# A conformer trunk step on one core: three projection tiles take un-normalised tokens

## The chip, the cores and the metric

The kernel runs on one core of a Trainium2 chip. The metric is device time of one execution in microseconds (us). Engines are named as in the profile: PE multiplies matrices, DVE, ACT and POOL work elementwise, SP issues most of the transfers.

## The reference

The program is one step of a two-layer encoder trunk (D = 1024 channels, 512 prompt tokens and 8 x 16 sample tokens, all in F32). Layer 0 is a conformer convolution module and a SwiGLU feed-forward net, layer 1 is attention and a feed-forward net. Only the start of layer 0 is touched by the change:

```
def rms_norm(x, g):
    return x * rsqrt(mean(x * x, axis=-1) + EPS) * g

def conv_module(h, hist, g, w_pw1, b_pw1, w_dw, b_dw, ln_g, ln_b, w_pw2, b_pw2):
    a, gate = split(rms_norm(h, g) @ w_pw1 + b_pw1, 2)
    glu = a * sigmoid(gate)
    full = concat([hist, glu])
    y = depthwise_conv(full, w_dw) + b_dw          # width 31, causal
    y = silu(layer_norm(y, ln_g, ln_b))
    return h + y @ w_pw2 + b_pw2, full[-30:]
```

The root `rsqrt(...)` is one number per token and the gain `g` one number per channel, so the root may be applied before the product with `w_pw1` or to its result.

## The kernel before

Channels lie on the partitions, tokens on the free axis. The 640 tokens are two groups: group 0 has 256 (the samples and the prompt's first 128), group 1 has 384. Each F32 product is made of three matmuls on halves that are split off (`mm3`, L167-172): high weight by high token (L170), low weight by high token (L171), high weight by low token (L172). Weights come through `wsplit` (L128-156): a transfer on SP into `raw`, the high half `whi` by ACT (L150), the low half `wlo` = raw - whi by DVE and POOL (L154). Each of these tiles has two buffers.

Group 0's normalisation (`rms`, L237-246, by `rstd_bc`, L221-231): eight squares, of which ACT makes four (L179) and DVE four (L182); DVE adds them up (L195); PE sums over the channels (L204, tile `w`, a PSUM tile named w2 in the code); DVE adds EPS (L226, `rst`), POOL takes the root (L230), PE spreads it over the partitions (L216). Then for each of the eight channel blocks DVE makes the normalised `n` (L243), ACT its high half (L159), DVE its low half (L160); both are tiles `x`. POOL does group 1's squares and sums; from there its normalisation is the same.

The order of the work is a list of steps, PLAN: "a0 y a1 a2 a4 x a3 a5 a6 l04 p04 l05 d0213 a7 b0 p05 b1 l07 p07 l06 b2 q00 s0 p06 n0 b3 b4 b5 d145 l13 w0 b7 r0 ...". `a`c is the gated projection `glu` (L369-396) of channel block c for group 0: two output tiles `mm` of 24 matmuls each (L170-172), tanh (L380) and identity (L383) on ACT, the gate product on DVE (L386) into the tile `gs`. `b`c is the same for group 1 (gate product L395 into `gp`). The depthwise convolution is made in three ways. `d` is on DVE, one multiply-add for each of 31 taps (L434, L437), into PSUM (`w`). `q` is on ACT and POOL (L409-417; POOL's add is L417). `l` and `p` are on PE: `l` writes a block of `gs` to DRAM (tile `sc`, L452) and reads it back with four shifts (tile `x4`, in the profile `x<-sc`, L455), beside a table `w4` that POOL makes (L444); `p` is then 64 matmuls (L469). `n0` is group 0's layer norm (`conv_ln`, L474-494): sums for the mean, then squares on ACT (L179), adds on POOL (L195), PE's sum (L204), the root (L226, L230), the spread (L216), and eight multiplies on DVE (L489), SiLU (L491) and split (L159, L160) that give the tokens of `w0`, the second projection `pw2` (its results are added to h at L506). `y` loads group 1's tokens, `x` normalises them, `r0` is the next normalisation of group 0, `f` a part of the feed-forward net.

A scheduler with a cost model makes from this list, the data dependences, the priorities (`tc.high_priority`) and the buffers one fixed order of instructions for each engine. An engine takes its instructions in that order and waits where one isn't ready, so a shift of one step can reorder others far behind it.

Of the kernel before, what the change touches and what calls it, by code (L numbers as in the profile page):

```python
# [71 lines left out]
V_NCONV, V_BPW1, V_BDW, V_LNG, V_LNB, V_BPW2 = 0, 8, 24, 32, 40, 48  # L72
# [5 lines left out]
def tile_trunk(ctx, tc, xT, vecs, hist, w_pw1, w_pw2, w_in0, w_out0, w_in1, w_out1,  # L78
               w_kq, w_v, w_o, rel, kc, vc, y_out, convp_out, convs_out, k_out, v_out):
    nc = tc.nc  # L80

    cst = ctx.enter_context(tc.tile_pool(name="cst", bufs=1))
# [37 lines left out]
    bca = cst.tile([P, NT], F32, name="bca", tag="bca")  # L120
# [4 lines left out]
    def col(base, i):  # L125
        return vec[:, base + i:base + i + 1]
# [94 lines left out]
    def rstd_bc(pieces, n, engs=SQ, cut=CUT, r2=None, eng=nc.gpsimd):  # L221
        st = w2t()
        nt = n // P
        r, v = colmean(st, [lambda s=s, e=e: square(s, n, e) for s, e in zip(pieces, engs)], n,
                       cut, "rst", eng)
        last["rst"] = nc.vector.tensor_scalar(out=r[:, :nt], in0=v, scalar1=EPS, scalar2=None,  # L226
                                              op0=ALU.add)
        if r2 is None:
            r2 = tp.tile([P, 4], F32, tag="rst2", name=nm("rst2"))
        nc.gpsimd.tensor_tensor(out=r2[:, :nt], in0=r[:, :nt], in1=mhalf[:, :nt], op=ALU.pow)  # L230
        return spread(st, r2, n), r2

    def hp(g, k):
        g0, n = GR[g]
        return h[:, k, g0:g0 + n]

    def rms(g, gain, engs=SQ, cut=CUT, eng=nc.gpsimd):  # L237
        n = GR[g][1]
        bc, _ = rstd_bc([hp(g, k) for k in range(KT)], n, engs, cut, None, eng)
        xh, xl = new_xs(g)  # L240
        for k in range(KT):
            t = tp.tile([P, 384], F32, tag="n1", name=nm("n1"), bufs=NB1)
            nc.vector.scalar_tensor_tensor(out=t[:, :n], in0=hp(g, k), scalar=col(gain, k),  # L243
                                           in1=bc, op0=ALU.mult, op1=ALU.mult)
            xsplit(t[:, :n], xh[:, k, :], xl[:, k, :])
        return xh, xl, None, None
# [21 lines left out]
    def xk(x, ks):  # L268
        return [(x[0][:, k, :], x[1][:, k, :]) for k in ks]
# [90 lines left out]
         cp.tile([P, KT, 384], F32, name="y1", tag="y")]  # L360

    w00 = wsplit(w_pw1[0], 16, P, cuts=4, pool=PL1[0][0])
    with tc.high_priority(offset=2 * HP):
        xs = [rms(0, V_NCONV, SSQ, SCUT, nc.vector), None]
    load_hist(0, 2)
    w01 = wsplit(w_pw1[1], 16, P, cuts=C01, pool=PL1[0][1])
    nc.scalar.dma_start(dwv, vecs[:, V_N:])

    def glu(c, g, wh, wl):  # L369
        n = GR[g][1]  # L370
        ps = []
        for ab in range(2):
            pt = mmt()
            mm3(pt[:, :n], [(wh[:, (ab * 8 + k) * P:(ab * 8 + k + 1) * P],
                             wl[:, (ab * 8 + k) * P:(ab * 8 + k + 1) * P]) for k in range(KT)],
                xk(xs[g], range(KT)))
            ps.append(pt[:, :n])
        with tc.high_priority(offset=HP):
            t = tp.tile([P, 384], F32, tag="t1", name=nm("t1"))
            nc.scalar.activation(out=t[:, :n], in_=ps[1], func=AF.Tanh, scale=0.5,  # L380
                                 bias=hb1[:, KT + c:KT + c + 1])
            a = tp.tile([P, 384], F32, tag="t2", name=nm("t2"))
            nc.scalar.activation(out=a[:, :n], in_=ps[0], func=AF.Identity, scale=0.5,  # L383
                                 bias=hb1[:, c:c + 1])
            if g == 0:
                nc.vector.scalar_tensor_tensor(  # L386
                    out=gs[:, c, :, HIST:SEG], in0=t[:, :n].rearrange("p (s w) -> p s w", w=SB),
                    scalar=1.0, in1=a[:, :n].rearrange("p (s w) -> p s w", w=SB),
                    op0=ALU.add, op1=ALU.mult)
                nc.gpsimd.tensor_copy(gs[:, c, 9:16, 14:30], gs[:, c, 8:15, 30:46])  # L390
                nc.gpsimd.tensor_copy(gs[:, c, 10:16, 0:14], gs[:, c, 8:14, 32:46])
                nc.gpsimd.tensor_copy(gp[:, c, 14:30], gs[:, c, 15, 30:46])
                nc.gpsimd.tensor_copy(gp[:, c, 0:14], gs[:, c, 14, 32:46])
            else:
                nc.vector.scalar_tensor_tensor(out=gp[:, c, HIST:HIST + 384], in0=t[:, :n], scalar=1.0,  # L395
                                               in1=a[:, :n], op0=ALU.add, op1=ALU.mult)
# [169 lines left out]
    xs = [rms_late(0, None), rms_late(1, None)]  # L566
# [280 lines left out]
    for p in range(NP):  # L847
# [424 lines left out]
```

## Time and profile before

| | us |
|---|---|
| median of 3 runs | 1551.79 (1549.15 to 1553.39) |
| profiled execution | 1551.3 |
| its span | 1549.5 |
| what lies around the span | 1.8 |
| PE busy in the span | 1471.7 (95%) |
| DVE busy | 1050.1 (68%) |
| ACT busy | 662.4 (43%) |
| POOL busy | 443.8 (29%) |

The granted TensorE clock has a mean of 0.984. A row of the timeline reads: start in the span, us from start to the end of its last instruction, engine (SPq is SP's queue of transfers), line, operation, result <- inputs, shapes, number of instructions in a row; in brackets the engine's idle time ahead of it and what ended that. Buffer numbers are left out of names, so `mm`, `x`, `w`, `raw` are each many tiles. A row of the windows reads: from:to, length, busy time and number of instructions of PE, PEld, DVE, ACT and POOL, granted clock, share of the time that transfers ran, GB/s.

### The profile page before, as it was taken

The page shows a single profiled execution, that of the slowest core. Times are in us where ns is not written, and L with a number is a line of the kernel's source. Part 1 is how long each engine was busy: PE and PEld are TensorE (multiplying, and loading weights), DVE is VectorE, ACT ScalarE, POOL GpSimd, SP SyncE. Part 2 cuts the span into 40 slices and gives each one's busy share as a digit, 9 for nine tenths or more (in the row PEclk, how much of TensorE's full clock was granted, in tenths as well). Part 3 has the DMA queues.
Part 4 walks back from the last instruction along what each step waited for, and adds up shares of the span by engine and source line. Part 5 has one row for each costly group of instructions (what it writes and reads, how often), then busy time and mean ns, then how long its engine had stood idle before and what let it go on. Part 6 is the DMA issues. An engine that isn't in the chain of part 4 may idle for free.

```text
span 1549.5 us, 26569 instructions
## 1 busy us (share of the span) xinstructions
PE 1471.7 (95%) x10770; PEld 1398.9 (90%) x10770; DVE 1050.1 (68%) x1863; ACT 662.4 (43%) x1173; POOL 443.8 (29%) x403
## 2 busy tenths in 40 slices
PE   5888998989999999999999999999989999999997
PEld 5878888989999999999988798886989999999997
DVE  6994999988555455457576767566796476476455
ACT  4544454535423323235454445443554244244244
POOL 6865568877501000001321211110411121121110
PEclk9999999999999999999999999998999999999998
DMA  7784434444421333433655545453103213213211
GB/s 236 234 228 142 137 113 159 148 157 153 147 82 55 129 116 129 135 118 126 202 183 201 174 140 205 133 175 114 55 28 109 82 56 109 82 55 109 82 55 68
DMA packets 59658, 199.95 MB, mean 129 GB/s; under 512 B 10128, under 2 KB 22672, under 8 KB 46736
## 3 DMA queue, kind: packets, MB, share of 16 engines
q1 hardware_dynamic: 59248, 197.96, 39.1%
q8 instruction: 84, 1.38, 0.4%
q10 hardware_dynamic: 288, 0.31, 0.1%
q14 instruction: 38, 0.31, 0.1%
HBM read 187.02 MB, written 11.22 MB: 128 GB/s over the span
## 4 chain that ended last, share of the span: by engine, by line
PE 71%; DVE 16%; ACT 3%; issue 3%; DMA 3%; POOL 2%; SPq 0%; POOLq 0%; DVEq 0%; ACTq 0%
PE mm L170 12%; PE mm L172 12%; PE mm L171 12%; PE pb L968 6%; DVE w L437 5%; DVE wlo L154 4%; PE pc L968 4%; PE pa L968 4%; PE pb L170 1%; PE pb L171 1%; PE pb L172 1%; PE pa L172 1%; PE pa L170 1%; PE pc L170 1%; PE pc L172 1%
## 5 line engine op out<-in xcount | busy, mean ns | idle before, releaser
L171 PE MATMUL mm<-x,wlo 128*128 128x256 f32 (+1 forms) x1344 | 416.8, 312 | 15.4 <-DVE wlo L154 14.9
L170 PE MATMUL mm<-x,whi 128*128 128x256 f32 (+1 forms) x1344 | 413.3, 312 | 6.4 <-ACT x L159 3.7
L172 PE MATMUL mm<-x,whi 128*128 128x256 f32 (+1 forms) x1344 | 412.7, 311 | 0.5
L150 ACT ACTIVATE whi<-raw 128x2048 fp32r<-128x2048 f32 (+2 forms) x117 | 197.7, 1694 | 232.6 <-PE mm L172 138.8
L171 PEld LDWEIGHTS mm<-x,wlo 128*128 128x128 f32 x1344 | 257.1, 192 | 18.7 <-DVE wlo L154 17.5
L170 PEld LDWEIGHTS mm<-x,whi 128*128 128x128 f32 x1344 | 254.5, 191 | 11.2 <-ACT x L159 4.1
L172 PEld LDWEIGHTS mm<-x,whi 128*128 128x128 f32 x1344 | 255.1, 191 | 2.9 <-DVE x L160 1.8
L154 DVE TENSOR_TENSOR wlo<-raw,whi 128x2048 fp32r<-128x2048 f32 (+5 forms) x117 | 214.0, 1832 | 62.2 <-ACT whi L150 61.2
L154 POOL TENSOR_TENSOR wlo<-raw,whi 128x1536 fp32r<-128x1536 f32 (+3 forms) x50 | 145.7, 2918 | 69.0 <-ACT whi L150 69.0
L913 POOL TENSOR_TENSOR raw<-raw 128x512 f32<-128x512 f32 x38 | 50.5, 1330 | 332.3 <-DVE raw L913 257.5
L171 PE MATMUL mm<-hid,wlo 128*128 128x256 f32 (+1 forms) x352 | 107.7, 308 | 6.6 <-DVE wlo L154 6.6
L172 PE MATMUL mm<-hid,whi 128*128 128x256 f32 (+1 forms) x352 | 105.8, 307 | 0.2
L170 PE MATMUL mm<-hid,whi 128*128 128x256 f32 (+1 forms) x352 | 104.6, 307 | 0.1
L437 DVE SCALAR_TENSOR_TENSOR w<-gp,dwv,w 128x384 f32<-128x384 f32 x180 | 103.9, 612 | 0.8
L195 POOL TENSOR_TENSOR acc<-sq,sq 128x384 f32<-128x384 f32 (+1 forms) x8 | 8.1, 1006 | 258.2 <-ACT sq L179 258.1
L171 PEld LDWEIGHTS mm<-hid,wlo 128*128 128x128 f32 x352 | 66.0, 188 | 7.8 <-DVE wlo L154 7.8
L417 POOL TENSOR_TENSOR y<-y,cvt 128x256 f32<-128x256 f32 (+1 forms) x60 | 69.3, 1154 | 6.3 <-ACT cvt L416 4.0
L172 PEld LDWEIGHTS mm<-hid,whi 128*128 128x128 f32 x352 | 65.7, 188 | 0.6 <-DVE hid L160 0.6
L159 ACT ACTIVATE whi<-raw 128x1024 fp32r<-128x1024 f32 x38 | 39.4, 1054 | 61.6 <-PE pc L172 18.1
L170 PEld LDWEIGHTS mm<-hid,whi 128*128 128x128 f32 x352 | 65.2, 188 | 0.4 <-ACT hid L159 0.3
L968 PE MATMUL pa<-x0f,whi 128*128 128x320 f32 x228 | 61.2, 316 | 2.5 <-DVE t L913 2.3
L195 POOL TENSOR_TENSOR acc<-acc,sq 128x384 f32<-128x384 f32 (+1 forms) x48 | 52.7, 1097 | 28.9 <-ACT sq L179 27.5
(317 smaller groups left out, 3391.4 us busy)
## 6 DMA issues: line engine op xcount, KB each, us to landing
raw<-in_w_in SPq DMA_DIRECT2D x62, 1024.0 KB
raw<-in_w_out SPq DMA_DIRECT2D x36, 768.0 KB
raw<-in_w_pw SPq DMA_DIRECT2D x22, 1024.0 KB
cache<-in_ck SPq DMA_DIRECT2D x32, 512.0 KB
cache<-in_cv SPq DMA_DIRECT2D x32, 512.0 KB
raw<-in_w_kq SPq DMA_DIRECT2D x8, 1024.0 KB
x<-sc SPq DMA_DIRECT2D x16, 368.0 KB
raw<-in_w_out SPq DMA_DIRECT2D x4, 1024.0 KB
```

Source lines behind the costliest of these rows:

```text
L150: nc.scalar.activation(out=hi[:, a:b], in_=raw[:, a:b], func=AF.Copy)
L154: eng.tensor_tensor(out=lo[:, a:b], in0=raw[:, a:b], in1=hi[:, a:b].bitcast(F32), op=ALU.subtract)
L159: nc.scalar.activation(out=hi, in_=src, func=AF.Copy)
L170: nc.tensor.matmul(ps, wh, xh, start=(i == 0), stop=False)
L171: nc.tensor.matmul(ps, wl, xh, start=False, stop=False)
L172: nc.tensor.matmul(ps, wh, xl, start=False, stop=(i == last))
L195: last["acc"] = eng.tensor_tensor(out=acc[:, :n], in0=prev, in1=s(), op=ALU.add)
L417: nc.gpsimd.tensor_tensor(out=y[g][:, c, :], in0=y[g][:, c, :], in1=pr[:, :n], op=ALU.add)
L437: nc.vector.scalar_tensor_tensor(out=dst, in0=src, scalar=wj, in1=dst, op0=ALU.mult, op1=ALU.add)
L913: ENG[e].tensor_tensor(out=out, in0=a, in1=b, op=op)
L968: nc.tensor.matmul(ps, a[:, c], b[:, k, :], start=(first and k == 0 and i == 0), stop=(k == 3 and i == 2), skip_group_check=not first)
```

## The change

All eight of group 0's squares are now on ACT. The projection tiles a0, a1 and a2 no longer take `x` but a new tile `xr`: the tokens times the gain, split into halves by eight ACT and eight DVE instructions, without the root. It lies in the buffer that group 1's `x` gets later. ACT copies the spread roots from PSUM into `bca`, and the six results of a0, a1, a2 are multiplied by it on DVE on their way from PSUM to tanh and identity. The normalised `x` of group 0 is still made, for a3 to a7. Lines of the changed kernel are 1 to 18 higher than those of the kernel before: L171 is L170 before, L205 is L204, L217 is L216, L180 is L179, L399 is L380, L401 is L383, L470 and L473 are L452 and L455; new are L242 (copy of the roots), L370 and L372 (split of `xr`), L397 (the multiplies).

```diff
-SSQ = 'avavavav'
+SSQ = 'aaaaaaaa'
+RAW = (0, 1, 2)
...
-    def rms(g, gain, engs=SQ, cut=CUT, eng=nc.gpsimd):
+    def rms(g, gain, engs=SQ, cut=CUT, eng=nc.gpsimd, keep=None):
...
+        if keep is not None:
+            nc.scalar.activation(out=keep, in_=bc, func=AF.Copy)
...
+    xr = cst.tile([P, 2, KT, 384], F32R, tag="x1", name="xr")
+    xr = xr[:, 0, :, 0:256], xr[:, 1, :, 0:256]
+    with tc.high_priority(offset=4 * HP):
+        for k in range(KT):
+            nc.scalar.activation(out=xr[0][:, k, :], in_=hp(0, k), func=AF.Copy,
+                                 scale=col(V_NCONV, k))
+            nc.vector.scalar_tensor_tensor(out=xr[1][:, k, :], in0=hp(0, k),
+                                           scalar=col(V_NCONV, k),
+                                           in1=xr[0][:, k, :].bitcast(F32), op0=ALU.mult,
+                                           op1=ALU.subtract)
     with tc.high_priority(offset=2 * HP):
-        xs = [rms(0, V_NCONV, SSQ, SCUT, nc.vector), None]
+        xs = [rms(0, V_NCONV, SSQ, SCUT, nc.vector, bca[:, 0:256]), None]
...
+        raw = g == 0 and c in RAW
...
-                xk(xs[g], range(KT)))
+                xk(xr if raw else xs[g], range(KT)))
...
+            if raw:
+                for i, o in ((1, t), (0, a)):
+                    nc.vector.tensor_tensor(out=o[:, :n], in0=ps[i], in1=bca[:, 0:n], op=ALU.mult)
+                    ps[i] = o[:, :n]
```

At the program's start PE's order before is the sum and the spread of the roots, then a0 (results `mm_28`, `mm_29`) and a1 (`mm_32`, `mm_33`) in turn, block by block of the normalised `x_16`:

```order
L204 MATMUL w2_4_123<-onec_80,acc_6_126 128x1 x2
L216 MATMUL w2_4_123<-ident_75,rst2_15_152 128x128 x2
L170 MATMUL mm_28_210<-x_16_156,whi_2_109 128x256
L171 MATMUL mm_28_210<-x_16_156,wlo_3_110 128x256
L170 MATMUL mm_29_235<-x_16_156,whi_2_109 128x256
L171 MATMUL mm_29_235<-x_16_156,wlo_3_110 128x256
L170 MATMUL mm_32_271<-x_16_156,whi_26_191 128x256
L171 MATMUL mm_32_271<-x_16_156,wlo_27_192 128x256
L170 MATMUL mm_33_296<-x_16_156,whi_26_191 128x256
L171 MATMUL mm_33_296<-x_16_156,wlo_27_192 128x256
L172 MATMUL mm_28_210<-x_16_156,whi_2_109 128x256
```

In the changed kernel PE starts with a0 on `xr`, and from its 36th row on the order reads (rows in between left out):

```order
L171 MATMUL mm_28_228<-xr_123,whi_2_109 128x256
L172 MATMUL mm_28_228<-xr_123,wlo_3_110 128x256
L173 MATMUL mm_28_228<-xr_123,whi_2_109 128x256
...
L172 MATMUL mm_29_253<-xr_123,wlo_3_110 128x256
L205 MATMUL w2_4_140<-onec_80,acc_6_143 128x1 x2
L173 MATMUL mm_29_253<-xr_123,whi_2_109 128x256
...
L173 MATMUL mm_32_291<-xr_123,whi_26_209 128x256
L217 MATMUL w2_4_140<-ident_75,rst2_15_169 128x128 x2
L171 MATMUL mm_32_291<-xr_123,whi_26_209 128x256
```

The sum of the roots moved behind 35 matmuls and the spread behind 66 of them (and the sum): both stood at the head of the queue. The multiplies of a0 and the normalised tokens, which a4 is the first to take, follow the spread.

On SP the four shifted reads of l04 (`x4`, L455 before) stood behind the transfer of a7's weights and now stand ahead of it.

Further on, on ACT around the second part of n0 (squares `sq_172` to `sq_180`; `t1_211` is the tanh of b5's gate, `whi_223` the high half of weights that come later). Before:

```order
L380 ACTIVATE t1_204_1562<-mm_203_1537,hb1_85 128x384
L150 ACTIVATE whi_218_1703<-raw_217_1702 128x2048
L179 ACTIVATE sq_178_1386<-y0_106 128x256
L179 ACTIVATE sq_179_1389<-y0_106 128x256
L383 ACTIVATE t2_212_1625<-mm_209_1573,hb1_85 128x384
L179 ACTIVATE sq_180_1392<-y0_106 128x256
L380 ACTIVATE t1_211_1623<-mm_210_1598,hb1_85 128x384
L150 ACTIVATE whi_223_1762<-raw_222_1761 128x2048
L491 ACT_TABLE_LOAD
L491 ACTIVATE n1_184_1405<-y0_106,vec_73 128x256
```

In the changed kernel the same place reads:

```order
L401 ACTIVATE t2_212_1648<-mm_209_1597,hb1_85 128x384
L180 ACTIVATE sq_175_1401<-y0_106 128x256
L180 ACTIVATE sq_176_1404<-y0_106 128x256
L180 ACTIVATE sq_177_1407<-y0_106 128x256
L180 ACTIVATE sq_178_1410<-y0_106 128x256
L399 ACTIVATE t1_211_1647<-mm_210_1622,hb1_85 128x384
L151 ACTIVATE whi_223_1786<-raw_222_1785 128x2048
L180 ACTIVATE sq_179_1413<-y0_106 128x256
L180 ACTIVATE sq_180_1416<-y0_106 128x256
L509 ACT_TABLE_LOAD
L509 ACTIVATE n1_184_1429<-y0_106,vec_73 128x256
```

The last two squares, which stood ahead of b5's tanh and of `whi_223`, now stand behind both. POOL's queue has the same change: `wlo_224`, its part of the low half of those weights, stood behind the root of n0 and now stands ahead of its last two adds. Before, and then in the changed kernel:

```order
L154 TENSOR_TENSOR wlo_219_1704<-raw_217_1702,whi_218_1703 128x1024
L195 TENSOR_TENSOR acc_173_1373<-acc_173_1373,sq_178_1386 128x256
L195 TENSOR_TENSOR acc_173_1373<-acc_173_1373,sq_179_1389 128x256
L195 TENSOR_TENSOR acc_173_1373<-acc_173_1373,sq_180_1392 128x256
L230 TENSOR_TENSOR rst2_182_1399<-rst_181_1397,mhalf_82 128x2
L154 TENSOR_TENSOR wlo_224_1763<-raw_222_1761,whi_223_1762 128x1024
```

```order
L196 TENSOR_TENSOR acc_173_1397<-acc_173_1397,sq_177_1407 128x256
L196 TENSOR_TENSOR acc_173_1397<-acc_173_1397,sq_178_1410 128x256
L155 TENSOR_TENSOR wlo_224_1787<-raw_222_1785,whi_223_1786 128x1024
L196 TENSOR_TENSOR acc_173_1397<-acc_173_1397,sq_179_1413 128x256
L196 TENSOR_TENSOR acc_173_1397<-acc_173_1397,sq_180_1416 128x256
L231 TENSOR_TENSOR rst2_182_1423<-rst_181_1421,mhalf_82 128x2
L155 TENSOR_TENSOR wlo_229_1846<-raw_227_1844,whi_228_1845 128x1024
```

The sum (PE), the root (DVE and POOL), the spread (PE) and the eight multiplies on DVE (L489) come behind those adds in both kernels. Of the work that stands ahead of these multiplies on DVE, the changed kernel has in addition three of group 1's convolution steps (L437 before) and one DVE part of `wlo_224`. Between the first `n` of group 1 and a7's gate product DVE has 14 convolution steps of group 0 and 2 other gate products, where it had 18 and 3. From the feed-forward net on, the orders are alike on every engine.

More of the change, by code (lines that the diff above doesn't have):

```diff
@@ L379, in glu @@
             t = tp.tile([P, 384], F32, tag="t1", name=nm("t1"))
+            a = tp.tile([P, 384], F32, tag="t2", name=nm("t2"))
+            if raw:
+                for i, o in ((1, t), (0, a)):
+                    nc.vector.tensor_tensor(out=o[:, :n], in0=ps[i], in1=bca[:, 0:n], op=ALU.mult)
+                    ps[i] = o[:, :n]
             nc.scalar.activation(out=t[:, :n], in_=ps[1], func=AF.Tanh, scale=0.5,
                                  bias=hb1[:, KT + c:KT + c + 1])
-            a = tp.tile([P, 384], F32, tag="t2", name=nm("t2"))
             nc.scalar.activation(out=a[:, :n], in_=ps[0], func=AF.Identity, scale=0.5,
```

## The prediction

> **What bounds the kernel now.** The page's first line is read first. PE is busy for 95% of the span, so what costs time is what makes PE wait; the rest is for the stages to say.
>
> ```profile
> PE 1471.7 (95%) x10770; PEld 1398.9 (90%) x10770; DVE 1050.1 (68%) x1863; ACT 662.4 (43%) x1173; POOL 443.8 (29%) x403
> ```
>
> The windows view then cuts the span where something is handed on: from the first `n` of group 1 to the gate of a7, from p07 to the end of b5, from the multiplies of n0 to 326 us, and from 400 us to the end.
>
> ```profile
> 51.77:81.41 29.64, 24.53 (x223) 21.96 (x222) 29.57 (x42) 17.20 (x30) 24.80 (x29) 0.94 0.92 240
> 103.81:149.10 45.29, 44.56 (x334) 40.19 (x334) 26.04 (x46) 14.19 (x23) 20.57 (x17) 0.96 0.49 136
> 152.00:326.00 174.00, 155.63 (x1226) 147.50 (x1226) 173.22 (x289) 86.58 (x122) 123.81 (x66) 0.96 0.43 140
> 400.00:1549.50 1149.50, 1126.16 (x8054) 1073.53 (x8053) 704.74 (x1325) 465.92 (x883) 162.83 (x192) 0.99 0.34 114
> ```
>
> PE is not the bound everywhere. In the first stage DVE works 29.57 of 29.64 us and PE waits for it; in the second PE works 44.56 of 45.29; in the third DVE 173.22 of 174. From 400 us on PE works 98% of the time in an unchanged order, so I take that part to be handed on as it is, only earlier or later. The change happens in the first 40 us, and what counts is what reaches 400 us through two stages that DVE bounds.
>
> **The start: PE is earlier, the roots are later.** The timeline of the first 45 us:
>
> ```profile
> 9.89 4.58 ACT L150 ACTIVATE whi<-raw 128x512 fp32r<-128x512 f32 x8
> ...
> 11.11 1.28 DVE L154 TENSOR_TENSOR wlo<-raw,whi 128x512 fp32r<-128x512 f32 x2
> ...
> 15.03 1.22 PE L216 MATMUL w<-ident,rst 128*128 128x128 f32 x4 [1.17 <-POOL rst L230]
> ...
> 16.29 0.87 DVE L243 SCALAR_TENSOR_TENSOR n<-h,vec,w 128x256 f32<-128x256 f32 x2 [1.21 <-PE w L216]
> ...
> 17.27 0.58 PE L170 MATMUL mm<-x,whi 128*128 128x256 f32 x1 [1.02 <-ACT x L159]
> 17.65 0.41 PE L171 MATMUL mm<-x,wlo 128*128 128x256 f32 x1
> 17.86 0.41 PE L170 MATMUL mm<-x,whi 128*128 128x256 f32 x1
> ...
> 22.57 0.28 PE L170 MATMUL mm<-x,whi 128*128 128x256 f32 x1
> 22.69 0.28 PE L171 MATMUL mm<-x,wlo 128*128 128x256 f32 x1
> ```
>
> Before, PE starts a0 at 17.27, behind the roots. Un-normalised tokens need only h and the gain: eight ACT and eight DVE instructions. The same forms on `x` give their prices:
>
> ```profile
> 16.80 0.81 ACT L159 ACTIVATE x<-n 128x256 fp32r<-128x256 f32 x2 [2.33 <-DVE n L243]
> ...
> 17.93 2.01 DVE L160 TENSOR_TENSOR x<-n,x 128x256 fp32r<-128x256 f32 x2
> ...
> 23.08 0.82 DVE L160 TENSOR_TENSOR x<-n,x 128x256 fp32r<-128x256 f32 x2
> ```
>
> That is 8 x 0.405 = 3.2 us of ACT and 8 x 0.41 = 3.3 us of DVE, up to 8 x 1.0 = 8.0 where the splits run as slowly as at 17.93. ACT has four more squares ahead of or among the weights as well. The first high half of weights moves from 9.89 to about 11.4 and the first low half, which PE needs at its second matmul, is ready at about 13.1 (11.11 + 0.68 for one of that pair + 1.3 for the `xr` splits ahead of it). So PE starts at 13.1 in place of 17.27: 4.2 us earlier, with bounds of 2 and 5.9 (first high half at 11.4, or the slow splits). For the first 5.3 us matmuls follow each other every 0.21 us (17.65, 17.86), from 22.57 on every 0.12; this slow beginning moves along and costs the same.
>
> What it costs is the root. Its sum now stands behind 35 matmuls and its spread behind 67 rows of PE. So the sum runs at about 20 (13.1, then 25 matmuls in the slow 5.3 us and 10 more at 0.12), and the spread, after 31 more at 0.12, at about 24, not 15.03. The normalised tokens start at 24.1, not 16.29: 7.8 us later.
>
> ```profile
> 36.01 0.38 PE L171 MATMUL mm<-x,wlo 128*128 128x256 f32 x1 [0.42 <-POOL wlo L154]
> ...
> 40.87 1.92 ACT L150 ACTIVATE whi<-raw 128x2048 fp32r<-128x2048 f32 x1 [1.45 <-DMA raw<-in_w_pw]
> ...
> 44.63 0.39 PE L170 MATMUL mm<-x,whi 128*128 128x256 f32 x2
> ...
> 51.77 1.13 DVE L243 SCALAR_TENSOR_TENSOR n<-h,vec,w 128x384 f32<-128x384 f32 x2
> ```
>
> Before, a2's second half waits for a low half at 36.01, ACT waits for the transfer of weights at 40.87, and a3 starts at 44.63. a0 and a1 now end at about 28 (96 matmuls from 13.1: 25 in 5.3 us, 71 at 0.12, and some 1.2 for the sum and the spread). But a2's weights go through ACT, DVE and POOL, and on ACT their high half (1.9) stands behind the first results of a0 and a1, which need the roots in `bca` (one ACT copy out of PSUM, about 0.48 like the tanh at 149.14 below, hidden beside DVE) and the first three multiplies, so it starts after 26. I take 31 to 33 for the low half, and a2 still ends near 36: the start's 4 us are spent there. a4 is the first that needs normalised tokens. From 24.1 DVE has eight `n` (0.435 each), eight low halves (0.41 to 1.0), six multiplies from PSUM (each about an `n`, 0.435: 2.6 us; bounds 0.36, a third of the 1.08 at 151.67 below, and 1.0, as at 17.93) and weight splits; by these durations the last low half is there at 39.4. PE waits in a4's first half until about 39.8, a4 ends at about 44.0 against 44.63, and the first `n` of group 1 comes 0.3 us earlier, at about 51.5. The four DVE squares removed (4 x 0.42) are paid for by six multiplies.
>
> **The first DVE stage: 2.4 us earlier.** The timelines of PE, DVE and SP:
>
> ```profile
> 67.03 5.24 PE L469 MATMUL mm<-x,w 128*32 128x256 f32 x64 [5.11 <-DMA x<-sc]
> ...
> 103.81 5.62 PE L469 MATMUL mm<-x,w 128*32 128x256 f32 x64 [5.43 <-DMA x<-sc]
> ```
>
> ```profile
> 80.16 0.55 DVE L160 TENSOR_TENSOR x<-n,x 128x384 fp32r<-128x384 f32 x1
> ...
> 81.41 0.41 DVE L386 SCALAR_TENSOR_TENSOR gs<-t,t 128x256 f32<-128x256 f32 x1
> ```
>
> ```profile
> 82.87 1.42 SPq L452 DMA_DIRECT2D sc<-gs  x2
> ...
> 91.74 1.74 SPq L455 DMA_DIRECT2D x<-sc  x4
> ```
>
> With the shifted reads of l04 ahead of a7's weights, p04's wait of 5.11 us at 67.03 goes. But b0 then needs group 1's tokens, the last low half of which DVE makes at 80.16, and p07 needs the gate of a7 (DVE, 81.41), the write at 82.87 and the reads at 91.74, which land when p07 starts at 103.81. That chain hangs on DVE. Ahead of a7's gate DVE has four convolution steps and one gate fewer:
>
> ```profile
> L437 DVE SCALAR_TENSOR_TENSOR w<-gs,dwv,w 128x256 f32<-128x256 f32 x20 | 9.5, 479 | 0.1
> L386 DVE SCALAR_TENSOR_TENSOR gs<-t,t 128x256 f32<-128x256 f32 x4 | 2.2, 546 | 0.0
> L160 DVE TENSOR_TENSOR x<-n,x 128x384 fp32r<-128x384 f32 x8 | 8.5, 1067 | 0.0
> ```
>
> A step has a mean of 0.479; back to back they follow each other every 0.40 (10 in 4.00 us):
>
> ```profile
> 83.16 8.36 POOL L417 TENSOR_TENSOR y<-y,cvt 128x256 f32<-128x256 f32 x8
> ...
> 85.97 4.00 DVE L437 SCALAR_TENSOR_TENSOR w<-gs,dwv,w 128x256 f32<-128x256 f32 x10
> ```
>
> 4 x 0.40 + 0.55 = 2.15 us, and with the 0.3 from the start p07 comes about 2.4 us earlier. The other DVE work beside POOL is where the error lies. The low halves `x` have a mean of 1067 ns in this stretch against 0.55 for one at 80.16, so 8 x 0.5 = 4 us of it is time in which they wait; another alignment with POOL can change the 2.4 to anything between 0 and 6.
>
> The Trainium skill, "SBUF — State Buffer", section "Who interferes with whom", says that a DVE instruction with two inputs in SBUF contends with a GpSimd instruction that reads SBUF, while one with at most one SBUF input does not. The trace agrees: the ten steps, whose second input lies in PSUM, take 0.40 each beside POOL's adds, and the `x` splits (both inputs in SBUF) take 0.55 to over 1. By this rule the five instructions that leave free just their own 2.15 us; if all of DVE's waiting shrank in proportion it would be about 2.7. The rule also speaks against the change, since the `xr` splits are of the contending kind.
>
> From p07 to the end of b5 PE is the bound (44.56 of 45.29), so the end of b5 moves from 149.10 to 146.7.
>
> **The layer norm n0: 7.7 us later.** The timeline around b5's end, and a pair of low halves ahead of it:
>
> ```profile
> 143.07 1.23 DVE L154 TENSOR_TENSOR wlo<-raw,whi 128x1024 fp32r<-128x1024 f32 x1 [0.72 <-ACT whi L150]
> ...
> 143.12 3.44 POOL L154 TENSOR_TENSOR wlo<-raw,whi 128x1024 fp32r<-128x1024 f32 x1 [1.18 <-ACT whi L150]
> ...
> 148.15 0.74 POOL L195 TENSOR_TENSOR acc<-acc,sq 128x256 f32<-128x256 f32 x1
> ...
> 149.14 0.58 ACT L380 ACTIVATE t<-mm,hb 128x384 f32<-128x384 f32 x1 [1.43 <-PE mm L172]
> ...
> 149.62 1.90 ACT L150 ACTIVATE whi<-raw 128x2048 fp32r<-128x2048 f32 x1
> ...
> 151.59 2.35 POOL L154 TENSOR_TENSOR wlo<-raw,whi 128x1024 fp32r<-128x1024 f32 x1 [0.72 <-ACT whi L150]
> ...
> 151.67 1.08 DVE L489 TENSOR_TENSOR y<-y,w 128x256 f32<-128x256 f32 x3 [0.65 <-PE w L216]
> ```
>
> Before, the last add (148.15 to 148.89) is done just ahead of b5's end, which is the end of the second window, 149.10; the sum, the root and the spread take 151.67 - 148.89 = 2.78 us more, and the multiplies start 2.57 us after b5. In the changed order the last two squares stand behind b5's tanh and the next weights' high half, and the last two adds behind POOL's part of the low half. Counted from b5's end: tanh and high half to 151.52, 2.42 us; POOL's low half 3.44, as where DVE makes its part at the same time (143.12; alone it was 2.35 at 151.59); two adds 2 x 0.74, with gaps 1.6; then 2.78. That is 10.3 us where it was 2.57: 7.7 later, or 6.6 with the short low half. PE's next instructions in its order are that sum and spread, and DVE stops at the multiplies. What PE could have hidden under it is gone: behind b5 stands only work that needs n0.
>
> **The second DVE stage: 3.1 us less to do.** While DVE would wait it has three more steps of group 1 and one more low half, which are then missing from the stage that it bounds:
>
> ```profile
> L437 DVE SCALAR_TENSOR_TENSOR w<-gp,dwv,w 128x384 f32<-128x384 f32 x180 | 103.9, 612 | 0.8
> ```
>
> With 1.23 for the low half (143.07), 3 x 0.612 + 1.23 = 3.1 us. Two small pieces that also change places around the end of the stage could make it 4.4.
>
> **The sum** goes against the profiled execution, 1551.3 us (span 1549.5 and 1.8 around it): -2.4 + 7.7 - 3.1 = +2.2, so 1553.5. The median of the runs is 0.5 higher, which gives 1554.0. A change of 0.3% (4.7 us: below 1547.1 or above 1556.4) is about what the measurement can tell from none.
>
> **The rivals.** *Faster:* the DVE stage passes on more. If p04's missing wait of 5.11 and the start's 0.6 at a3 reach p07 whole (5.7), n0's low half is the short one less its overlap with the squares (5.3), and 4.4 us are done ahead, the sum is 5.3 - 5.7 - 4.4 = -4.8: 1547.0. For it speaks how much of that stage is waiting beside POOL, against it that DVE is full there. *Slower:* the root reaches the normalised tokens too late for a4 and a3. They then keep PE waiting beyond 44.63, the weights' buffers come free later, and group 1's `n` starts near 56 in place of 51.77, some 4 us later, of which the five missing instructions give 2.15 back, so p07 is 2 us late: 7.7 + 2 - 3.1 = +6.6, so 1558.4. It gives slower by over 0.3% as soon as p07 is later than before (7.7 + 0.1 - 3.1 = 4.7). For it speaks the spread behind 67 rows. *The change doesn't do what it says:* the splits run at the slow 1.0 us, PE starts at about 17 as before, and everything behind the root is 4 us later: 7.7 + 4 - 3.1 = +8.6, 1560.4.
>
> **How the numbers follow.** The forecast gets 0.42 (0.38 of it within the 0.3%, 0.04 above), the faster rival 0.30 (0.22 below, 0.08 within, since 1547.0 lies at the bound), the slower one 0.22 (0.19 above, 0.03 within), the last 0.06 (above). So faster 0.22, same 0.49, slower 0.29. The forecast's own range is 1550 to 1556.5 (6.6 for 7.7, 4.4 for 3.1 and 4 for 2.4 at one end, 0 for 2.4 at the other); 8 in 10 reach to the rivals on both sides with 1.5 us of margin below and 0.6 above, 1545.5 to 1559.0; the last case is left out.
>
> **What would show it.** Right: PE's first matmul at about 13, the spread near 24, PE waiting in a4; p04 without a wait; p07 at about 101.4; the multiplies of n0 some 10 us after b5's end; from 400 us on the same rows 2 us later. Wrong: a handover at p07 that moves by more than 4 us either way, or n0's multiplies within 5 us of b5's end.

## The result, and the profile after

The changed kernel is slower: 1567.88 us (1565.54 to 1575.83, 4 runs) against 1552.59 (1549.15 to 1554.24, 4 runs), a ratio of 1.0119 with a 95% interval of 1.0098 to 1.014. The forecast was 1554.0 with a range of 1545.5 to 1559.0 and "same" as the likeliest: the sign of the sum, +2.2, was right, its size was not. The medians lie 15.3 us apart (0.98%), at the lower end of that interval. The profiled execution took 1569.17 us, 17.9 more than that of before, and its span grew from 1549.5 to 1567.0: 17.5 us, which the rest of the text takes apart.

The page's first line shows no engine with 17 us more to do, so the loss is waiting:

```profile
PE 1476.4 (94%) x10770; PEld 1402.5 (90%) x10770; DVE 1055.6 (67%) x1873; ACT 666.6 (43%) x1186; POOL 443.4 (28%) x403
```

PE's timeline of the start has only those rows where it began, waited or made the roots (the lines are those of the changed kernel):

```profile
10.30 0.58 PE L171 MATMUL mm<-xr,whi 128*128 128x256 f32 x1 [10.30 <-ACT whi L151]
12.72 0.58 PE L172 MATMUL mm<-xr,wlo 128*128 128x256 f32 x1 [1.84 <-DVE wlo L155]
...
18.78 0.50 PE L205 MATMUL w<-onec,acc 128*128 128x1 f32 x4
...
22.88 0.61 PE L217 MATMUL w<-ident,rst 128*128 128x128 f32 x4
...
29.14 0.50 PE L171 MATMUL mm<-xr,whi 128*128 128x256 f32 x2 [2.23 <-ACT whi L151]
30.72 0.58 PE L172 MATMUL mm<-xr,wlo 128*128 128x256 f32 x1 [1.08 <-DVE wlo L155]
...
41.92 0.38 PE L173 MATMUL mm<-x,whi 128*128 128x256 f32 x1 [1.73 <-DVE x L161]
43.07 0.39 PE L173 MATMUL mm<-x,whi 128*128 128x256 f32 x1 [0.53 <-DVE x L161]
```

Up to a2 this went as forecast: PE is in full work from 12.72 (13.1 forecast), the spread comes at 22.88 (24), and a2 waits for its high half until 29.14 and for its low half until 30.72 (31 to 33). a4 waits for normalised tokens, as forecast, but until 43.07, not 39.8. The windows, between the same events as those of before:

```profile
55.49:82.23 26.74, 23.74 (x208) 21.27 (x208) 26.58 (x37) 16.39 (x28) 21.49 (x24) 0.94 0.89 244
104.57:151.68 47.11, 45.12 (x332) 40.34 (x332) 26.94 (x45) 13.00 (x20) 16.61 (x13) 0.95 0.46 132
163.01:337.00 173.99, 150.79 (x1170) 142.19 (x1171) 172.06 (x280) 83.81 (x120) 118.81 (x64) 0.95 0.38 126
416.20:1567.00 1150.80, 1125.20 (x8055) 1072.69 (x8053) 705.70 (x1325) 465.92 (x883) 162.65 (x192) 0.99 0.34 114
```

Their ends tell where the time went. The gate of a7 comes at 82.23 (81.41 before), p07 at 104.57 (103.81), the end of b5 at 151.68 (149.10), n0's multiplies at 163.01 (151.67), the last window begins 16.2 us later, and its length grew by 1.3. The first half of n0's tail, from ACT, POOL, PE and DVE:

```profile
152.81 1.90 ACT L151 ACTIVATE whi<-raw 128x2048 fp32r<-128x2048 f32 x1
154.61 0.71 ACT L180 ACTIVATE sq<-y 128x256 f32<-128x256 f32 x2
154.78 3.38 POOL L155 TENSOR_TENSOR wlo<-raw,whi 128x1024 fp32r<-128x1024 f32 x1 [1.19 <-ACT whi L151]
158.13 1.51 POOL L196 TENSOR_TENSOR acc<-acc,sq 128x256 f32<-128x256 f32 x2
159.70 1.02 PE L205 MATMUL w<-onec,acc 128*128 128x1 f32 x4 [8.02 <-POOL acc L196]
...
163.01 2.74 DVE L507 TENSOR_TENSOR y<-y,w 128x256 f32<-128x256 f32 x8 [0.26 <-PE w L217]
```

Read from below: DVE waits for PE's spread, PE waited 8.02 us for POOL's last add, POOL's adds stood behind 3.38 us of weight split, and that behind ACT's 1.90 us. The multiplies come 163.01 - 151.68 = 11.3 us behind b5's end; 10.3 was forecast.

The stage behind, from n0's multiplies to DVE's first subtraction of n1, before and after:

```profile
151.67:349.86 198.19, 175.93 (x1388) 167.66 (x1389) 190.69 (x303) 95.29 (x132) 142.57 (x72) 0.96 0.43 139
```

```profile
163.01:364.37 201.36, 176.46 (x1388) 167.67 (x1389) 188.07 (x299) 93.89 (x131) 138.38 (x71) 0.96 0.40 132
```

DVE has 2.6 us less to do there (190.69 to 188.07), about the 3.1 of the forecast, and the stage is still 3.2 us longer: DVE's idle time grew from 7.5 to 13.3.

### The profile page after: what moved, and what is told of

Its sections match the earlier page's. It is cut to its first block, busy times and chain, and to the rows that moved or that the text cites. A ratio compares the mean times of both kernels' runs of the same rounds, so it can differ in the third digit from the quotient of the medians.

```text
span 1567.0 us, 26602 instructions
## 1 busy us (share of the span) xinstructions
PE 1476.4 (94%) x10770; PEld 1402.5 (90%) x10770; DVE 1055.6 (67%) x1873; ACT 666.6 (43%) x1186; POOL 443.4 (28%) x403
## 4 chain that ended last, share of the span: by engine, by line
PE 71%; DVE 13%; DMA 5%; POOL 4%; ACT 4%; issue 3%; SPq 0%; DVEq 0%; ACTq 0%; POOLq 0%
PE mm L171 13%; PE mm L172 12%; PE mm L173 12%; PE pb L986 6%; DVE w L455 4%; PE pc L986 4%; PE pa L986 4%; DVE wlo L155 3%; PE pb L171 1%; PE pb L173 1%; PE pb L172 1%; PE pa L173 1%; PE pa L171 1%; PE pc L173 1%; PE pc L171 1%
## 5 line engine op out<-in xcount | busy, mean ns | idle before, releaser
L172 PE MATMUL mm<-x,wlo 128*128 128x384 f32 (+1 forms) x1296 | 404.3, 313 | 20.3 <-DVE wlo L155 18.6
L171 PE MATMUL mm<-x,whi 128*128 128x384 f32 (+1 forms) x1296 | 400.3, 313 | 3.3 <-ACT x L160 1.9
L173 PE MATMUL mm<-x,whi 128*128 128x384 f32 (+1 forms) x1296 | 400.0, 312 | 2.5 <-DVE x L161 2.3
L172 PEld LDWEIGHTS mm<-x,wlo 128*128 128x128 f32 x1296 | 247.8, 191 | 24.3 <-DVE wlo L155 22.0
L155 DVE TENSOR_TENSOR wlo<-raw,whi 128x2048 fp32r<-128x2048 f32 (+5 forms) x117 | 217.8, 1864 | 62.4 <-ACT whi L151 62.3
L171 PEld LDWEIGHTS mm<-x,whi 128*128 128x128 f32 x1296 | 245.5, 191 | 7.7 <-issue 2.9
L173 PEld LDWEIGHTS mm<-x,whi 128*128 128x128 f32 x1296 | 246.4, 191 | 4.6 <-DVE x L161 3.5
L171 PE MATMUL mm<-hid,whi 128*128 128x256 f32 (+1 forms) x352 | 106.0, 311 | 1.6 <-ACT whi L151 0.9
L455 DVE SCALAR_TENSOR_TENSOR w<-gp,dwv,w 128x384 f32<-128x384 f32 x180 | 104.2, 611 | 1.0
L171 PEld LDWEIGHTS mm<-hid,whi 128*128 128x128 f32 x352 | 66.1, 191 | 2.6 <-ACT whi L151 1.1
L143 ACT ACTIVATE whi<-raw,vec 128x128 fp32r<-128x128 f32 (+1 forms) x160 | 52.4, 410 | 17.0 <-PE mm L173 15.3
```

The source lines that it names most:

```text
L143: nc.scalar.activation(out=hi[:, a:b], in_=raw[:, a:b], func=AF.Copy, scale=gain)
L155: eng.tensor_tensor(out=lo[:, a:b], in0=raw[:, a:b], in1=hi[:, a:b].bitcast(F32), op=ALU.subtract)
L171: nc.tensor.matmul(ps, wh, xh, start=(i == 0), stop=False)
L172: nc.tensor.matmul(ps, wl, xh, start=False, stop=False)
L173: nc.tensor.matmul(ps, wh, xl, start=False, stop=(i == last))
L455: nc.vector.scalar_tensor_tensor(out=dst, in0=src, scalar=wj, in1=dst, op0=ALU.mult, op1=ALU.add)
```

## The experiments

Ratios are to runs of the kernel before on the same chip, with the 95% interval; the changed kernel itself has 1.0119. Times in the expectations were written against a before of 1551 to 1552; in these sessions it had medians of 1549.4 to 1552.2. Theory Q says that n0's slip in the queues makes most of the loss, theory R that the late roots do.

**e1 and e2: n0's adds and last two squares on DVE.** In the changed kernel (e1) and, as a control, in the kernel before (e2):

```diff
-        bc, _ = rstd_bc([y[g][:, c, :] for c in order], n)
+        bc, _ = (rstd_bc([y[g][:, c, :] for c in order], n, 'aaaaaavv', CUT, None, nc.vector)
+                 if g == 0 else rstd_bc([y[g][:, c, :] for c in order], n))
```

> The changed kernel, with n0's adds and its last two squares on DVE, no longer behind the weights' high half on ACT and the low half on POOL. Theory Q (the order of n0's tail costs 8 of the 16 us): the multiplies of n0 start 3 to 5 us behind b5's end, not 11.3, and the time falls by 6 to 9 us, to 1559 to 1562. Theory R (the late roots at the start cost it all, n0 only shows the slip): the time falls by less than 3 us, to 1565 to 1568. Theory M (the wait moves on, to the weights or the convolution on DVE behind n0): the multiplies come early and the time falls by less than 3 us all the same.

> The same edit of n0 in the kernel before, as its control. Theory Q: n0's tail is 2.6 us there and can give little, so within 2 us of before, 1550 to 1555. If it gains 6 us or more here too, the edit is a gain by itself and says nothing on the change.

e1 gave 1562.11 us, ratio 1.0073 (1.0047 to 1.01); e2 1549.24, ratio 0.9993 (0.9976 to 1.001). PE's sum and spread and DVE's multiplies of e1:

```profile
152.81 0.61 PE L205 MATMUL w<-onec,acc 128*128 128x1 f32 x4 [2.00 <-DVE acc L196]
154.71 1.22 PE L217 MATMUL w<-ident,rst 128*128 128x128 f32 x4 [1.30 <-POOL rst L231]
```

```profile
156.08 2.73 DVE L508 TENSOR_TENSOR y<-y,w 128x256 f32<-128x256 f32 x8
```

PE waits 2.00 in place of 8.02, and the multiplies start at 156.08 in place of 163.01. Counted from b5's end (150.81) that is still 5.3 us, 2.57 in the kernel before. Of the 6.9 us some 7 arrive by the ratios (0.46%, with intervals that just overlap), about 6.7 by the spans (1567.0 to 1560.3). In the profiles only 3.4 of them are there at n1's first subtraction (360.99 in place of 364.37), since the stage behind n0 takes 204.9 us; the rest arises from n1 on, where the order is the same. The edit by itself is worth nothing (e2). So n0's tail is real and, by the ratios, some 7 us of it lie on the path, but 0.7% remain.

**e3: the squares alone.** The kernel before with one line of the change:

```diff
-SSQ = 'avavavav'
+SSQ = 'aaaaaaaa'
```

> The kernel before with only the first part of the change: all eight squares of group 0 on ACT. Theory Q: n0 has the order of before, so within 2 us of before, 1550 to 1555. Rival: four squares more on ACT hold up the first weights' high half by 1.7 us and this reaches the end, 1554 to 1557.

1551.57 us, ratio 1.0006 (0.9988 to 1.0025). This part of the change costs nothing; the un-normalised tokens bring the loss.

**e4, e6: one tile and four tiles.** The changed kernel with another list of tiles:

```diff
-RAW = (0, 1, 2)
+RAW = (0,)
```

> The changed kernel with a0 alone on un-normalised tokens: two multiplies in place of six, the spread behind 50 rows of PE, and n0's tail in the order of the changed kernel. Theory Q: the tail still costs 8 us: 1560 to 1567. Theory R: with a third of the late work the start costs a third or less: 1551 to 1557.

1564.65 us, ratio 1.0092 (1.0059 to 1.0125). And with RAW = (0, 1, 2, 4):

> The changed kernel with a4 on un-normalised tokens as well, so that the first tile that needs the normalised ones comes 5 us later; eight multiplies in place of six. If a4's wait for the late tokens is what the start hands on, a3 starts 1 to 2 us earlier than in the changed kernel and the time falls by 1 to 2 us (1564 to 1567). Theory P: weights and DVE bound it, so the same within 2 us (1565 to 1570).

1569.52 us, ratio 1.0116 (1.0094 to 1.0138). In both, n0's tail has the order of the changed kernel, and from its first subtraction to its multiplies it takes 20.24 us, as in the changed kernel; in the kernel before it is 14.66. The loss does not follow the number of tiles. It is there as soon as one tile takes un-normalised tokens.

**e5: without the low half.** The changed kernel without the eight DVE splits (high half used twice):

```diff
-    xr = xr[:, 0, :, 0:256], xr[:, 1, :, 0:256]
+    xr = xr[:, 0, :, 0:256], xr[:, 0, :, 0:256]
...
-            nc.vector.scalar_tensor_tensor(out=xr[1][:, k, :], in0=hp(0, k),
-                                           scalar=col(V_NCONV, k),
-                                           in1=xr[0][:, k, :].bitcast(F32), op0=ALU.mult,
-                                           op1=ALU.subtract)
```

> The changed kernel without the eight DVE instructions that make the low half of the un-normalised tokens; the high half is multiplied in its place, so the work of a0, a1 and a2 on PE is the same and their result is not. The rest of every engine's order stays. Theory P (the start's 5 us of new DVE work only shift PE's start; the handover at a7's gate hangs on the late roots, weights and DVE's order): the gate of a7, 0.8 us late now, comes 0 to 2 us earlier, and the time stays at 1564 to 1569. Theory S (the new splits are the cost of the start and it reaches the end): the gate comes 3 to 5 us earlier and the time falls by 3 to 5 us, to 1562 to 1565.

1569.29 us, ratio 1.0113 (1.0082 to 1.0145). The roots are 2.2 us earlier (spread at 20.66), and the gate of a7 comes at 82.57 all the same, where the changed kernel has 82.23. Taking the new splits out gives nothing back: up to that gate DVE is busy for 67.3 us with 97 instructions, 66.5 with 105 in the changed kernel, because other work takes longer (the weights' low halves of 1024 took 13.5 us in place of 10.8).

**e7 and e8: b7 ahead of w0.** In the changed kernel (e7) and in the kernel before (e8):

```diff
-... d145 l13 w0 b7 r0 ...
+... d145 l13 b7 w0 r0 ...
```

> The changed kernel with b7 ahead of w0 in the list of steps, so that PE has 9 us of work while n0's tail is on its way. Theory B (behind n0 the feed-forward net's backlog on PE sets the end of the DVE stage, and PE's idle 11 us behind b5 are what is lost): the time falls by 6 to 9 us, to 1558 to 1562. Theory D (DVE's work alone sets the end of that stage, as the prediction had it): less than 3 us, 1565 to 1569.

> The same exchange of b7 and w0 in the kernel before, where PE idles some 4 us behind b5. Theory B: 2 to 4 us faster than before, 1546 to 1550. Theory D: within 1.5 us of before.

e7 gave 1570.35 us, ratio 1.0118 (1.0089 to 1.0148); e8 1559.58, ratio 1.0055 (1.0034 to 1.0077). PE's sum and spread and DVE's multiplies of e7:

```profile
159.73 0.50 PE L205 MATMUL w<-onec,acc 128*128 128x1 f32 x4
...
161.26 0.71 PE L217 MATMUL w<-ident,rst 128*128 128x128 f32 x4 [1.04 <-POOL rst L231]
```

```profile
162.21 1.08 DVE L507 TENSOR_TENSOR y<-y,w 128x256 f32<-128x256 f32 x3
```

PE no longer waits for the add, since b7 fills the time; the multiplies come at 162.21, as late as ever, and nothing is gained. Theory B falls in its simple form: PE's idle time at n0 is not what is lost. In e8 the spread now stands behind b7 (PE at 157.73, multiplies at 158.38 in place of 151.67), and it gets slower, which neither theory forecast. Both fit the reading that the lateness of n0's tokens is what costs, but the exchange reorders the queues behind it as well, so they do not show it.

**e9: the slip alone.** The kernel before, with n0 listed two steps later and no un-normalised tokens:

```diff
-... s0 p06 n0 b3 b4 b5 ...
+... s0 p06 b3 b4 n0 b5 ...
```

> The kernel before, with the step n0 listed behind b4 in place of ahead of b3 and nothing else: normalised tokens everywhere, the start as before, but n0's last three squares on ACT behind b5's tanh and the weights' high half, as the last two are in the changed kernel. Theory Q (the slip of n0 in the queues is most of the loss, whatever brought it about): the multiplies of n0 start 8 to 12 us later than before and the time is 1558 to 1564. Theory R (the late roots are the loss): within 3 us of before.

1563.61 us, ratio 1.0076 (1.0061 to 1.0091). The same rows as above, now of e9:

```profile
149.90 1.90 ACT L150 ACTIVATE whi<-raw 128x2048 fp32r<-128x2048 f32 x1
...
151.70 0.71 ACT L179 ACTIVATE sq<-y 128x256 f32<-128x256 f32 x2
...
151.88 3.38 POOL L154 TENSOR_TENSOR wlo<-raw,whi 128x1024 fp32r<-128x1024 f32 x1 [1.73 <-ACT whi L150]
...
155.22 2.33 POOL L195 TENSOR_TENSOR acc<-acc,sq 128x256 f32<-128x256 f32 x3
...
157.59 1.01 PE L204 MATMUL w<-onec,acc 128*128 128x1 f32 x4 [8.21 <-POOL acc L195]
...
160.97 1.41 DVE L489 TENSOR_TENSOR y<-y,w 128x256 f32<-128x256 f32 x4 [0.32 <-PE w L216]
```

With the start of before, untouched, n0's place in the queues alone makes PE wait 8.21 us, puts the multiplies 9.3 us later (160.97 against 151.67) and costs 0.76% of the change's 1.19%. This is the strongest evidence for theory Q: a slip of n0 costs about 12 us without any un-normalised token. It is not the same slip, so these 12 us are not measured as a part of the 18: here three adds stand behind the low half and n0's first subtraction is 8.2 us later than before (145.25 against 137.01), in the changed kernel it is two adds and 5.8 us (142.77). The stage behind n0 gets longer here too, 203.1 us of which DVE idles 14.6.

**e10 and e11: n0 earlier.** n0 ahead of b2 in the changed kernel (e10) and in the kernel before (e11):

```diff
-... l06 b2 q00 s0 p06 n0 b3 ...
+... l06 q00 s0 p06 n0 b2 b3 ...
```

> The changed kernel with the step n0 listed ahead of b2, so that 9 us of PE's work more lie between n0's squares and the first tile that needs them. Theory Q: the multiplies of n0 start no later than in the kernel before, 10 us of the loss go, and the time is 1554 to 1560. Theory R: 1564 to 1568. If only the second part of n0 hurts, as e1 had it, 1559 to 1562.

> The same move of n0 in the kernel before, as the control of e10: n0's tail is 2.6 us there, so 1546 to 1553; what it gains here is not to be counted for e10.

1571.98 us, ratio 1.0132 (1.0117 to 1.0147), and 1569.56, ratio 1.0112 (1.0097 to 1.0127). Both came out slower than expected, though the multiplies of e10 start at 158.12, 4.9 us earlier than in the changed kernel. PE's rows of p06, first of e10, then of e11:

```profile
120.30 5.00 PE L487 MATMUL mm<-x,w 128*32 128x256 f32 x64 [9.31 <-DMA x<-sc]
```

```profile
118.30 5.27 PE L469 MATMUL mm<-x,w 128*32 128x256 f32 x64 [9.18 <-ACT y L440]
```

b2, which PE had to do ahead of p06, now stands behind n0, and PE waits 9.31 and 9.18 us there, where it is 1.99 in the changed kernel and 0.72 in the kernel before. So n0 has a place from which it is bad to move it either way, and e10 does not tell the theories apart.

**e12: less work for DVE.** The kernel before with three taps fewer in group 1's convolution:

```diff
-        for j in range(W):
+        for j in range(W if g == 0 else W - 3):
```

> The kernel before with 28 taps in place of 31 in group 1's convolution on DVE: 18 steps of 0.53 us (9.5 us) of DVE's work are left out of the stage behind n0, so the output isn't the reference's. Theory D (DVE's work sets that stage's end): n1's first subtraction comes 8 to 10 us earlier, and the time is 1540 to 1544. Theory B (PE's backlog sets it): less than 4 us, 1546 to 1551, and DVE waits for PE at the stage's end by what was taken out.

1549.34 us, ratio 0.9976 (0.9964 to 0.9988). The stage behind n0, its window and DVE's and PE's longest waits:

```profile
151.90:344.62 192.72, 171.39 (x1349) 163.69 (x1350) 177.12 (x283) 94.15 (x130) 138.91 (x71) 0.96 0.43 139
```

```profile
PE mm L171 <- DVE wlo L154: 17.8, 14, 2.6
...
DVE h L303 <- PE mm L172: 6.0, 3, 2.2
...
DVE t L288 <- PE mm L172: 4.5, 1, 4.5
```

DVE has 13.6 us less to do than before (190.69 to 177.12); the stage gets 5.5 us shorter and the time 3.6. The rest turns into idle time of DVE, most of it waiting for PE (15.6 us idle, 7.5 before). So that stage is not bounded by DVE's work alone, though DVE was busy for 99.6% of the window that I had read. PE waits for low halves, and DVE makes those in its turn between convolution steps. I read this as a ring, in which work taken from one place shortens only what lies on the ring there; no run shows that by itself.

**e13 and e14: POOL out of w0's weights.** In the changed kernel (e13) and in the kernel before (e14):

```diff
-PL1 = ((0, 2, 2, 2, 2, 2, 2, 2), (0, 0, 0, 3, 0, 0, 0, 2))
-PL2 = (2, 2)
+PL1 = ((0, 2, 2, 2, 2, 2, 2, 2), (0, 0, 0, 3, 0, 0, 0, 0))
+PL2 = (0, 2)
```

> The changed kernel with the low halves of w0's and b7's weights made on DVE alone, POOL's half taken over. POOL's queue is then free for n0's adds, and all of n0's squares stand ahead of b5's tanh and the weights' high half again. Theory Q with contention: n0's multiplies start 3 to 6 us behind b5's end in place of 11, the stage behind does not get longer since DVE's low halves no longer wait for POOL, and the time falls by 8 to 12 us, to 1556 to 1560. Theory Q without contention: DVE has 5 us more to do, 1560 to 1564. Theory R: 1565 to 1570.

> The same in the kernel before, as the control of e13. With contention: DVE's whole low half (2048) takes some 2.3 us, its half beside POOL 2.1 to 2.8, so nothing is lost: 1549 to 1553. Without: 5 us more of DVE, 1554 to 1557.

1558.23 us, ratio 1.0051 (1.0032 to 1.007), and 1551.76, ratio 1.0005 (0.9983 to 1.0027). PE's sum of n0 and the stage behind it, of e13:

```profile
158.36 0.82 PE L205 MATMUL w<-onec,acc 128*128 128x1 f32 x4 [2.46 <-POOL acc L196]
```

```profile
162.66:359.90 197.24, 174.29 (x1388) 166.06 (x1389) 188.67 (x301) 93.76 (x131) 135.87 (x68) 0.97 0.42 140
```

PE waits 2.46, not 8.02, n0's tail takes 15.66 us (162.66 less 147.00, its first subtraction), and the stage is as short as before, 197.24. By the ratios more than half of the change's loss is gone by an edit that the kernel before does not feel. The profile does not put it all at n0: the multiplies come 6.8 us behind b5's end in place of 11.3, but b5 ends at 155.90, 4.2 us later than in the changed kernel with the same order ahead of it, so at 162.66 they are no earlier than there. Of the 10.8 us between the spans 4.1 are the stage and 6.3 arise from n1 on, where the orders are alike.

**e15 and e16: POOL out of the feed-forward weights.** In the changed kernel (e15) and in the kernel before (e16):

```diff
-PFA = 3
-PFB = 3
+PFA = 0
+PFB = 0
```

> The changed kernel with the low halves of the feed-forward net's weights behind n0 on DVE alone (POOL had three quarters); n0's tail stays as it is in the changed kernel. If the stage behind n0 was stretched by DVE's waiting for POOL, that stage gets 3 to 8 us shorter and the time falls by 3 to 6 us, to 1561 to 1565. If not, DVE has more to do: up to 22 splits by 1 us more each, and the time rises by 5 us or more.

> The same in the kernel before, as the control of e15: with contention 2 to 5 us faster, 1546 to 1549; without, slower by 5 us or more.

1579.22 us, ratio 1.0186 (1.0144 to 1.0227), and 1571.89, ratio 1.014 (1.0102 to 1.0178): POOL's share is worth some 20 us to the kernel before. The low halves on DVE from 150 to 350 us, first of e16, then of the kernel before:

```profile
L154 DVE TENSOR_TENSOR wlo<-raw,whi 128x2048 fp32r<-128x2048 f32 x17 | 38.9, 2288 | 10.0 <-ACT whi L150 10.0
```

```profile
L154 DVE TENSOR_TENSOR wlo<-raw,whi 128x512 fp32r<-128x512 f32 x16 | 30.3, 1894 | 3.0 <-ACT whi L150 3.0
```

A whole low half costs DVE 2288 ns, a quarter of one beside POOL 1894 in the mean, though one alone takes 0.69 us, as DVE's timeline of the kernel before shows:

```profile
338.81 0.69 DVE L154 TENSOR_TENSOR wlo<-raw,whi 128x512 fp32r<-128x512 f32 x1 [1.51 <-ACT whi L150]
```

So the waiting for POOL is large, but without POOL it is worse. With the feed-forward weights made this way the change costs only the difference of e15 and e16, some 0.5%, and their intervals overlap.

## Why the prediction was wrong, point by point

**The start** did what the working said up to a2, and p04's wait of 5.11 us is gone, as forecast. The first step that failed is the one behind it: "by these durations the last low half is there at 39.4", a4 ends at about 44.0, and the first `n` of group 1 comes "0.3 us earlier, at about 51.5". Two of DVE's rows, and then that `n`:

```profile
35.24 0.42 DVE L397 TENSOR_TENSOR t<-mm,bca 128x256 f32<-128x256 f32 x1 [1.97 <-PE mm L173]
...
39.69 3.32 DVE L161 TENSOR_TENSOR x<-n,x 128x256 fp32r<-128x256 f32 x2
...
55.49 1.13 DVE L246 SCALAR_TENSOR_TENSOR n<-h,vec,w 128x384 f32<-128x384 f32 x2
```

The working's list of DVE's work leaves out the gate products of a0 and a1 (1.04 us at 27.38, 1.23 at 31.26) and every wait: a multiply of a2's result stands ahead of a4's last tokens and waits 1.97 us for PE. With two slow low halves behind it (3.32 us) the last one is there at 43.0, not 39.4, and the `n` starts 4.0 us later than forecast, 3.7 later than before. DVE has 69 instructions ahead of it where it had 56: ten from the start's new work, and two convolution steps and a gate product that stood behind it before.

**The first DVE stage** was then to give 2.15 us: "Ahead of a7's gate DVE has four convolution steps and one gate fewer". Counted from that `n`, as I had done, the stage did get 2.9 us shorter (29.64 to 26.74). But two of the steps and the gate had not gone, they had only changed sides. Counted from the program's start, DVE has 105 instructions ahead of that gate where it had 97: four squares and two convolution steps fewer, eight splits and six multiplies more. The gate is 0.8 us late, where 2.4 early was forecast. Over nine profiles each (the two kernels, e1 to e16 by their start) it comes at 81.5 to 85.3 with the changed start, 82.8 in the mean, and at 78.9 to 81.4 without, 80.6 in the mean: 2.2 us later. What PE gained ahead of a2 went into a2's wait for weights and a4's wait for tokens. Which part of the start costs the 2.2 is open: without the new splits the gate is no earlier (e5), and with a4 on `xr` too it comes at 81.47 (e6).

**From p07 to b5's end** I had PE as the bound and no change. It took 47.11 us in place of 45.29: p06 waits 1.99 us for its shifted reads (at 121.03), where it waited 0.72 for ACT before. Together the end of b5 is 2.6 us late, not 2.4 early: 5.0 us of the miss.

**n0's tail** was right in mechanism, rows and nearly in size: 8.8 us (11.33 less 2.57) for a forecast of 7.7. The high half starts 1.13 us behind b5's end, not 0.52, and from the last add to the multiplies it is 3.4 us, not 2.8. e9 shows such a tail without the change's start, e1 and e13 take a part of it away. A second part of the slip, which POOL's adds hide, stands neither in the prediction nor in the orders shown: PE's spread of n0's mean now stands behind 93 of the 144 matmuls between p06 and n0's sum, where it stood behind 75, so n0's first subtraction comes 8.9 us ahead of b5's end, not 12.1. It shows in e1, where POOL is out of the way and the multiplies are still 2.7 us later behind b5's end than before.

**The second DVE stage** is the other step that failed: three more steps and a low half done ahead, "which are then missing from the stage that it bounds", 3.1 us. DVE's work did shrink by 2.6. But a busy share of 99% was not a bound (e12): DVE's idle time grew by 5.8 us in its place, and the stage got longer. DVE's waits in it, first of before, then of after (time in all, times, longest):

```profile
DVE t L288 <- PE mm L172: 3.6, 2, 3.4
DVE wlo L154 <- ACT whi L150: 3.0, 2, 1.5
```

```profile
DVE wlo L155 <- ACT whi L151: 5.7, 4, 2.2
DVE t L291 <- PE mm L173: 3.8, 1, 3.8
DVE h L306 <- PE mm L173: 1.7, 2, 1.4
DVE h L524 <- PE mm L173: 1.1, 1, 1.1
```

That is 3.0 us more for PE and 2.7 more for ACT's high halves. In the first half of the stage some of DVE's instructions themselves got longer. Up to the second part of the feed-forward net (from n0's spread, 97.4 us after and 92.3 before, with the same 84 convolution steps), these groups of DVE took longer, first of before, then of after:

```profile
L154 DVE TENSOR_TENSOR wlo<-raw,whi 128x512 fp32r<-128x512 f32 x6 | 11.9, 1985 | 0.0
L154 DVE TENSOR_TENSOR wlo<-raw,whi 128x1024 fp32r<-128x1024 f32 x4 | 8.5, 2118 | 0.0
...
L395 DVE SCALAR_TENSOR_TENSOR gp<-t,t 128x384 f32<-128x384 f32 x2 | 1.1, 551 | 0.0
```

```profile
L155 DVE TENSOR_TENSOR wlo<-raw,whi 128x512 fp32r<-128x512 f32 x6 | 13.3, 2224 | 0.0
L155 DVE TENSOR_TENSOR wlo<-raw,whi 128x1024 fp32r<-128x1024 f32 x3 | 8.4, 2800 | 0.0
...
L413 DVE SCALAR_TENSOR_TENSOR gp<-t,t 128x384 f32<-128x384 f32 x2 | 4.1, 2050 | 0.0
```

They read two inputs from SBUF, and by the rule of the Trainium skill named in the prediction ("SBUF — State Buffer", "Who interferes with whom") such an instruction contends with a GpSimd instruction that reads SBUF; the trace agrees: of the two gate products one takes 0.55 us as before, the other 3.55 from 220.97 on, beside a weight split of POOL from 220.64 to 224.11, and the convolution steps, whose second input is in PSUM, take 613 and 614 ns. But the four splits `hid` of the same stretch, which also read two inputs from SBUF, took 3.1 us in place of 4.4, and over the whole stage the low halves of 512 took 26.7 us in place of 30.3. So contention moved time within the stage; that it made the stage longer is not shown. The stage is 198 us in the kernel before and in e2 and e3, 200 to 206 in the changed kernel, e1, e4, e5, e6 and e9, and 197 in e13, where POOL has no part in w0's weights. e13 changed the queue's order too, so it does not settle that. Since e9 has the longer stage with the start of before, the late roots are not needed for it; what makes it longer is open. The miss here is 6.3 us.

**From n1 on** I had no change; the span shows another 3.0 us (14.5 late at n1's first subtraction, 17.5 at the end). In e3, whose order behind the start is that of before, that stretch took 3.9 us more in the profile (1203.5 against 1199.6), though by its runs e3 is no slower than before, so I take most of the 3.0 for the difference between two executions. The granted clock fits that: in the 50 us behind n1's first subtraction it was 1.00 before, 0.97 in the changed kernel and in e3.

In sum 2.6 + 8.8 + 3.2 + 3.0 = 17.5 with the rounding, where -2.4 + 7.7 - 3.1 stood. The two stages that were to give 5.5 us back (2.4 and 3.1) took 5.8 (2.6 and 3.2). The rival on the slower side had the right path for its loss (group 1's `n` near 56, a handover at p07 that is not earlier) but let the 3.1 us stand, which is why even its 1558.4 is too low.

## What to carry to other kernels

Where a scheduler writes a fixed order for each engine, a change at the start can cost most at a place that it does not touch: look along every queue for steps that slipped behind a long, unrelated instruction, and try that slip alone in the kernel before. To compare DVE's work "ahead of" an event, count from the program's start, not from another event that may have moved in the same queue, and count the waits too: e5 has 97 instructions ahead of a7's gate, as before, and the gate is no earlier than in the changed kernel. And a stage in which an engine is busy for 99% is not yet bounded by it: take some of its work away and see whether the time follows.

## What the runs showed of the hardware

A quarter of a weight's low half (512 elements) cost DVE 1.9 us in the mean beside POOL's three quarters and 0.69 alone, so sharing such work saved DVE only 0.4 us of the 2.29 that the whole costs, and yet taking POOL out made the kernel before 1.4% slower. The slow beginning of PE, 5.3 us of matmuls every 0.21 us before, lasted 4.4 us in the changed kernel (12.72 to 17.14, behind one lone matmul at 10.30).
